# Delta rule on one core: diagonal blocks of 16 instead of 32 by substitution, the corner between them by products

## The chip, the cores and the metric

The program runs on one core of one Trainium2 chip. The time is device microseconds of one execution. Five engines matter: TensorE (PE; its weight loads are shown apart as PEld), VectorE (DVE), ScalarE (ACT), GpSimd (POOL) and SyncE (SP), which here issues DMAs. Each engine takes its instructions strictly in the order in which they stand in its queue; between engines, semaphores hold an instruction until what it reads is there.

## The reference

The program computes two blocks of a small model over 512 tokens. Only one part of the second block matters here, the gated delta rule, for eight heads of width 128. Its inner part, cut:

```python
decay = jnp.exp(jnp.where(causal, gc[..., :, None] - gc[..., None, :], -jnp.inf))
lmat = jnp.where(strict, jnp.einsum('bnhcd,bnhed->bnhce', k_beta, k) * decay, 0.0)
t_inv = lax.linalg.triangular_solve(eye + lmat, ..., left_side=True, lower=True, unit_diagonal=True)
u = jnp.einsum('bnhce,bnhed->bnhcd', t_inv, v_beta)
w = jnp.einsum('bnhce,bnhed->bnhcd', t_inv, k_beta * jnp.exp(gc)[..., None])
...
def step(state, xs):
    v_new = u_c - jnp.einsum('bhcd,bhde->bhce', w_c, state)
    o_c = jnp.einsum(..., q_c, state) + jnp.einsum(..., a_c, v_new)
    state = state * gl[..., None, None] + jnp.einsum('bhcd,bhce->bhde', k_c, v_new)
```

For each chunk of tokens a triangular matrix with ones on its diagonal has to be inverted (`t_inv`); then a state runs from chunk to chunk. The reference takes chunks of 64; the kernel takes chunks of 128, which gives the same result, so that a head has four chunks and each needs the inverse of a 128 x 128 triangle.

## The kernel before

The function that matters is `block2`. Its loop over eight heads, `for h in range(8)` (line 1444), emits for each head:

- Four projections by `K.gemm`, 24 products each (lines 313, 314 and 316, here called gemm products). Their weights come from `K.wtiles`: a DMA, a rounded copy `whi` on ScalarE (line 301), and the rest `wlo` by a subtraction on GpSimd (line 303). Three of the projections pass a convolution, `cv`, on VectorE (line 1290).
- The norm of q and k: transposes of `kq` into the PSUM buffers `ta`, sums of squares on ScalarE, some twenty small VectorE instructions (`rs_v` to `nbk`); `V` (line 1491); the decays `E`.
- Products of k with k and q (line 1502), of which VectorE makes `NU`, the strict triangle with its sign, and `Aq` (lines 1505 and 1507). All four chunks lie side by side in a tile.
- The inverse `D` of `I - NU`. Its four diagonal blocks of 32, of all four chunks at once, are gathered into `nd` [128, 4, 32] by four ScalarE copies and inverted by substitution in 31 steps of three VectorE instructions: a shuffle that gives every lane of 32 the row `i` (line 1519), a product (1521), a sum into `dc` (1522). A step i works on 4 x (31 - i) columns, from 124 down to 4.
- Then blocks are doubled, 32 to 64 to 128: ScalarE copies `dc` into `D`; VectorE transposes it into `Dt` (1527); products (1531), ScalarE copies `P1`, products (1538), ScalarE copies into `D`, transposes (1543), ScalarE copies `Dt6`, products (1548), ScalarE copies `P16`, products (1553), and VectorE copies the last corner into `D` (1554).
- The state over four chunks: products with `D` (1567), `vn` on ScalarE, products with `Aq`, `kd` and `kq`, and `Wc`, `O` and `S` on VectorE; at last the norm of `O`, its transposes, and `ya`.

The order on each engine is not this one. A scheduler with its own model of costs lays the instructions of neighbouring heads into each other: gemm products of later heads stand between the small products of this head, and while VectorE runs the substitution of one head, it also does the convolutions of a later head and the state of the head before. Two buffers stand for `D` (`Ds[h % 2]`), for `nd` and for most tiles of a head. Behind the heads come eight more projections, with no part in the delta rule, and an output stage that needs `ya` of all heads.

## Time and profile before

| | |
|---|---|
| runs shown | 2583.11, 2585.26, 2588.78 us; median 2585.26 us |
| profiled execution, first to last instruction | 2582.1 us |
| PE busy | 2421.6 us (94%) |
| VectorE busy | 1515.6 us (59%) |
| ScalarE busy | 986.7 us (38%) |
| GpSimd busy | 701.3 us (27%) |
| mean granted clock of TensorE | 0.972 |

The profile gives, for one execution, every instruction's engine, line, start and duration. A busy PE is not PE at its peak, since matmuls are pipelined and their ends are modelled. The granted clock is a share of 2.4 GHz; it takes two levels, 1.2 and 2.4 GHz, so that a mean between 0.5 and 1 says which part of a stretch ran at the lower one. The time of the profiled execution that is given is its span alone; the median of the runs lies 3.2 us above it. The shares are means over the whole program: the loop over heads fills the time from about 2110 to 2475 us. Many instructions in a product of two f32 operands are recorded twice, so a product there counts as two records.

### The profile page before, as it was taken

Reading aid. Unit: us, or ns where it says so; the run is one execution under the profiler, and the core shown is the slowest. Engines: PE = TensorE matmul, PEld = TensorE weight load, DVE = VectorE, ACT = ScalarE, POOL = GpSimd, SP = SyncE. Lnnn points to the kernel's source line nnn. Section 1 sums busy time; section 2 is a strip of 40 time slices with the busy share of each in tenths; the row PEclk is TensorE's granted clock in tenths of the full one; section 3 lists DMA queues with packets and bytes.
Section 4 is the critical chain, followed back from the end, with each engine's and each line's share of the span. In section 5 each row is a group of like instructions: output and inputs, shape, how many; then the busy total and the mean of one; then the engine's idle time right before and its main releaser. Section 6 shows DMA issues by size and latency. Waiting matters only on the chain.

```text
span 2582.1 us, 33519 instructions
## 1 busy us (share of the span) xinstructions
PE 2421.6 (94%) x12640; PEld 1977.7 (77%) x12640; DVE 1515.6 (59%) x3638; ACT 986.7 (38%) x1920; POOL 701.3 (27%) x313
## 2 busy tenths in 40 slices
PE   8899898999999999989989999999999998988897
PEld 4788777877888888867887788887777786666676
DVE  5857789788384452466875523335331248897854
ACT  4344433242132222344653423333444345554431
POOL 1221112222332223220013344443233342222242
PEclk9899999999999999999999999999999999998998
DMA  7311224325454331221002232223111231111131
GB/s 266 110 49 66 86 66 155 135 82 170 140 164 146 100 106 62 72 77 48 31 34 98 74 106 84 94 102 135 59 56 62 80 117 54 58 54 54 50 114 65
DMA packets 65889, 237.68 MB, mean 92 GB/s; under 512 B 7584, under 2 KB 10560, under 8 KB 50752
## 3 DMA queue, kind: packets, MB, share of 16 engines
q1 hardware_dynamic: 62848, 229.61, 26.2%
q10 hardware_dynamic: 2880, 5.94, 0.7%
q8 instruction: 100, 1.64, 0.3%
q14 instruction: 61, 0.50, 0.1%
HBM read 229.21 MB, written 6.31 MB: 91 GB/s over the span
## 4 chain that ended last, share of the span: by engine, by line
PE 70%; DVE 18%; ACT 3%; issue 2%; DMA 2%; DVEq 0%; ACTq 0%
PE mm L313 14%; PE mm L314 14%; PE mm L316 14%; PE mm L1134 4%; PE mm L1135 4%; PE mm L1136 4%; DVE ada_acc L365 2%; DVE dt L1521 2%; DVE dc L1522 2%; DMA adaraw<-in_ada_dram 2%; DVE row L1519 1%; PE lv L927 1%; DVE cv L1290 1%; PE mm L324 1%; PE mm L325 1%
## 5 line engine op out<-in xcount | busy, mean ns | idle before, releaser
L303 POOL TENSOR_TENSOR wlo<-wraw,whi 128x1024 fp32r<-128x1024 f32 (+2 forms) x301 | 686.8, 2283 | 1720.3 <-ACT whi L301 1486.1
L301 ACT ACTIVATE whi<-wraw 128x1024 fp32r<-128x1024 f32 (+2 forms) x301 | 299.8, 997 | 838.4 <-PE mm L314 361.4
L313 PE MATMUL mm<-fhi,whi 128*128 128x512 f32 (+1 forms) x1056 | 374.7, 358 | 1.9 <-ACT fhi L451 1.9
L314 PE MATMUL mm<-flo,whi 128*128 128x512 f32 (+1 forms) x1056 | 360.7, 357 | 0.0
L316 PE MATMUL mm<-fhi,wlo 128*128 128x512 f32 (+1 forms) x1056 | 321.6, 357 | 0.0
L313 PE MATMUL mm<-h2h,whi 128*128 128x512 f32 x584 | 243.8, 419 | 1.6 <-ACT h2h L451 1.6
L314 PE MATMUL mm<-h2l,whi 128*128 128x512 f32 x584 | 242.4, 416 | 0.0
L316 PE MATMUL mm<-h2h,wlo 128*128 128x512 f32 x584 | 241.3, 414 | 0.0
L313 PEld LDWEIGHTS mm<-fhi,whi 128*128 128x128 f32 x1056 | 198.5, 188 | 49.2 <-ACT fhi L451 2.7
L314 PEld LDWEIGHTS mm<-flo,whi 128*128 128x128 f32 x1056 | 198.7, 188 | 31.5 <-DVE flo L452 0.3
L365 DVE SCALAR_TENSOR_TENSOR ada_acc<-adaraw,silu_c,ada_acc 128x512 f32<-128x512 f32 x182 | 175.6, 965 | 33.1 <-DMA adaraw<-in_ada_dram 30.9
L316 PEld LDWEIGHTS mm<-fhi,wlo 128*128 128x128 f32 x1056 | 176.2, 190 | 17.7
L1134 PE MATMUL mm<-ffh,whi 128*128 128x512 f32 (+1 forms) x528 | 188.1, 358 | 1.1 <-ACT ffh L331 1.1
L1135 PE MATMUL mm<-ffl,whi 128*128 128x512 f32 (+1 forms) x528 | 188.7, 358 | 0.0
L1136 PE MATMUL mm<-ffh,wlo 128*128 128x512 f32 (+1 forms) x528 | 187.8, 357 | 0.0
L313 PE MATMUL mm<-hhi,whi 128*128 128x512 f32 (+1 forms) x488 | 173.9, 360 | 5.6 <-ACT F L884 3.7
L314 PE MATMUL mm<-hlo,whi 128*128 128x512 f32 x488 | 166.2, 359 | 0.7 <-DVE hlo L452 0.6
L1109 DVE SCALAR_TENSOR_TENSOR fft<-mm,sv,fft 128x511 f32<-128x511 f32 x66 | 43.5, 658 | 187.3 <-ACT fft L1108 187.3
L1138 DVE SCALAR_TENSOR_TENSOR x<-mm,mod_l,x 128x512 f32<-128x512 f32 x64 | 48.1, 751 | 165.3 <-PE mm L1136 165.3
L316 PE MATMUL mm<-hhi,wlo 128*128 128x512 f32 (+1 forms) x488 | 144.0, 362 | 0.0
L313 PEld LDWEIGHTS mm<-h2h,whi 128*128 128x128 f32 x584 | 113.9, 195 | 23.9 <-issue 1.8
L314 PEld LDWEIGHTS mm<-h2l,whi 128*128 128x128 f32 x584 | 114.4, 196 | 22.9 <-issue 1.6
(551 smaller groups left out, 4761.4 us busy)
## 6 DMA issues: line engine op xcount, KB each, us to landing
adaraw<-in_ada_dram SPq DMA_DIRECT2D x208, 256.0 KB, 3.0
wraw<-in_w_up_dram SPq DMA_DIRECT2D x44, 1024.0 KB, 4.7
wraw<-in_w_b_dram SPq DMA_DIRECT2D x40, 1024.0 KB, 4.9
wraw<-in_w_ev_dram SPq DMA_DIRECT2D x14, 1024.0 KB, 4.8
wraw<-in_w_dn_dram SPq DMA_DIRECT2D x16, 768.0 KB, 4.3
wraw<-in_w_dn_dram SPq DMA_DIRECT2D x16, 640.0 KB, 3.9
adaraw<-in_ada_dram SPq DMA_DIRECT2D x16, 512.0 KB, 10.0
wraw<-in_w_evo_dram SPq DMA_DIRECT2D x4, 1024.0 KB, 5.0
```

The costliest lines, as they stand in the source:

```text
L301: nc.scalar.activation(hi, raw[:, g], AF.Copy)
L303: nc.gpsimd.tensor_sub(lo, raw[:, g], hi.bitcast(F32))
L313: self.nc.tensor.matmul(p, whi[:, k, :], hhi[:, k, c0:c0 + n], start=k == 0, stop=False)
L314: self.nc.tensor.matmul(p, whi[:, k, :], hlo[:, k, c0:c0 + n], start=False, stop=False)
L316: self.nc.tensor.matmul(p, wlo[:, k, :], hhi[:, k, c0:c0 + n], start=False, stop=k == KT - 1)
L365: nc.vector.scalar_tensor_tensor(acc, raw, c[:, kk:kk + 1], acc, op0=OP.mult, op1=OP.add)
L1134: nc.tensor.matmul(p, whi[:, k, :], fhi[:, c:c + n], start=k == 0, stop=False)
L1135: nc.tensor.matmul(p, whi[:, k, :], flo[:, c:c + n], start=False, stop=False)
L1136: nc.tensor.matmul(p, wlo[:, k, :], fhi[:, c:c + n], start=False, stop=k == gn - 1)
L1138: nc.vector.scalar_tensor_tensor(xx[:, j], p, m[:, 40 + j:41 + j], xx[:, j], op0=OP.mult, op1=OP.add)
L1521: nc.vector.tensor_tensor(t, row, dc[:, :, i:i + 1].to_broadcast([128, 4, m]), op=OP.mult)
L1522: nc.vector.tensor_tensor(dc[:, :, i + 1:], dc[:, :, i + 1:], t, op=OP.add)
```

## The change

The four blocks of 32 on the diagonal are each cut into two blocks of 16 and a corner of 16 x 16. Both blocks of 16 go through one chain of 15 steps: the shuffle now gives the upper 16 lanes of each 32 their row `i` and the lower 16 their row `16 + i`. For this `nd` is first folded, by two masks, into `n16` [128, 4, 16]. The corner of every block of 32 is cut out by a mask (`nk`) and spread by four ScalarE copies into a block-diagonal tile `N` [128, 4, 128], of which there are two, zeroed once. After the chain `dh` is unfolded into `dc` by the two masks. Two groups of four products, `p1` and `p2`, multiply the inverses of the two blocks of 16 with the corner: `Dk` is the transpose of `dc`, `PX` spreads the result of `p1` block by block over 128 columns while reading it out of PSUM, and the result of `p2` is added to `dc`. From there on, from `D` and `Dt` to the end, the code is as before. The constants `d32` become one tile `dk`. The other edits take out comments, so that the lines of later code are shifted by some places.

```diff
-    A['d32'] = (i[:, None] % 32 == np.arange(32)).astype(f)
+    dk = np.zeros((128, 54), f)
+    dk[:, :16] = i[:, None] % 16 == np.arange(16)
+    dk[:, 16] = i % 32 < 16
+    dk[:, 17] = i % 32 >= 16
+    dk[:, 18:50] = (i[:, None] % 32 < 16) & (np.arange(32) >= 16)
+    dk[:, 50:] = i[:, None] // 32 == np.arange(4)
...
+        d16, m0, m1, corner, blk = dk[:, :16], dk[:, 16:17], dk[:, 17:18], dk[:, 18:50], dk[:, 50:54]
...
+        Ns = [dp.tile([128, 4, 128], F32, name=f"N{i}") for i in range(2)]
...
+            n16 = dp.tile([128, 4, 16], F32, name="n16", tag="n16", bufs=2)
+            nc.vector.tensor_scalar(n16, nd[:, :, 0:16], m0, None, op0=OP.mult)
+            nc.vector.scalar_tensor_tensor(n16, nd[:, :, 16:32], m1, n16, op0=OP.mult, op1=OP.add)
+            nk = dp.tile([128, 4, 32], F32, name="nk", tag="nk", bufs=2)
+            nc.vector.tensor_tensor(nk, nd, corner[:, None].to_broadcast([128, 4, 32]), op=OP.mult)
+            for b in range(4):
+                r = slice(32 * b, 32 * b + 32)
+                ND(N[r, :, r], nk[r])
+            dh = dp.tile([128, 4, 16], F32, name="dh", tag="dh", bufs=2)
+            nc.vector.tensor_copy(dh, d16[:, None].to_broadcast([128, 4, 16]))
+            for i in range(15):
+                m = 15 - i
+                row = dp.tile([128, 4, m], F32, name="row", tag="row", bufs=4)
+                nc.vector.stream_shuffle(row, n16[:, :, i + 1:], [i] * 16 + [16 + i] * 16)
+                t = dp.tile([128, 4, m], F32, name="dt", tag="dt", bufs=2)
+                nc.vector.tensor_tensor(t, row, dh[:, :, i:i + 1].to_broadcast([128, 4, m]), op=OP.mult)
+                nc.vector.tensor_tensor(dh[:, :, i + 1:], dh[:, :, i + 1:], t, op=OP.add)
             dc = dp.tile([128, 4, 32], F32, name="dc", tag="dc", bufs=2)
-            nc.vector.tensor_copy(dc, d32[:, None].to_broadcast([128, 4, 32]))
-            for i in range(31):
-                m = 31 - i
-                row = dp.tile([128, 4, m], F32, name="row", tag="row", bufs=4)
-                nc.vector.stream_shuffle(row, nd[:, :, i + 1:], [i] * 32)
-                t = dp.tile([128, 4, m], F32, name="dt", tag="dt", bufs=2)
-                nc.vector.tensor_tensor(t, row, dc[:, :, i:i + 1].to_broadcast([128, 4, m]), op=OP.mult)
-                nc.vector.tensor_tensor(dc[:, :, i + 1:], dc[:, :, i + 1:], t, op=OP.add)
+            for k, m in enumerate((m0, m1)):
+                nc.vector.tensor_scalar(dc[:, :, 16 * k:16 * k + 16], dh, m, None, op0=OP.mult)
+            Dk = dp.tile([128, 4, 32], F32, name="Dk", tag="Dk", bufs=2)
+            nc.vector.transpose(Dk.rearrange("p a b -> p (a b)"), dc.rearrange("p a b -> p (a b)"))
+            p1 = K.pt("tb")
+            for c in range(4):
+                nc.tensor.matmul(p1[:, c * 32:c * 32 + 32], N[:, c], Dk[:, c], start=True, stop=True)
+            PX = dp.tile([128, 4, 4, 32], F32, name="PX", tag="PX", bufs=1)
+            nc.vector.tensor_tensor(PX, p1[:, None, :128].rearrange("p o (c j) -> p c o j", c=4).to_broadcast([128, 4, 4, 32]),
+                                    blk[:, None, :, None].to_broadcast([128, 4, 4, 32]), op=OP.mult)
+            p2 = K.pt("tb")
+            for c in range(4):
+                nc.tensor.matmul(p2[:, c * 32:c * 32 + 32], PX[:, c].rearrange("p b j -> p (b j)"), dc[:, c], start=True, stop=True)
+            nc.vector.tensor_tensor(dc, dc, p2[:, :128].rearrange("p (a b) -> p a b", a=4), op=OP.add)
```

Up to the first head's substitution each engine's order is that of before; from there the scheduler lays the heads into each other in another way. VectorE's queue of before, at the end of the fifth head's substitution (an entry is line, operation, result and sources, result's size; `tb` and `ta` are PSUM buffers):

```order
L1527 STREAM_TRANSPOSE Dt<-dc 128x128
L1491 TENSOR_TENSOR V<-ta,ik 128x512
L1507 TENSOR_TENSOR Aq<-ta,E 128x256
L1290 SCALAR_TENSOR_TENSOR cv<-mm,sv,cv 128x511
L1515 COPY dc<-d_14818 128x128
L1290 SCALAR_TENSOR_TENSOR cv<-mm,sv,cv 128x510
L1505 SCALAR_TENSOR_TENSOR NU<-ta,nbk,E 128x128 x2
L1507 TENSOR_TENSOR Aq<-ta,E 128x256
L1290 SCALAR_TENSOR_TENSOR cv<-mm,sv,cv 128x509
L1554 COPY D_16811<-tb 64x4x64
L1519 STREAM_SHUFFLE row<-nd 128x124
```

The same place in the changed kernel, where the lines 1544, 1559 and 1586 are the transposes `Dk` and `Dt` and the last copy into `D`, and line 1554 is now the sum of `p2` into `dc`:

```order
L1544 STREAM_TRANSPOSE Dk<-dc 128x128
L1532 COPY dh<-dk 128x64
L1549 TENSOR_TENSOR PX<-tb,dk 128x512
L1554 TENSOR_TENSOR dc<-dc,tb 128x128
L1559 STREAM_TRANSPOSE Dt<-dc 128x128
L1586 COPY D_16811<-tb 64x4x64
L285 TENSOR_SCALAR rs_v<-dss 128x8
L287 TENSOR_SCALAR rs_i<-rs_v 128x8
L289 TENSOR_SCALAR rs_j<-rs_i 128x8
L293 TENSOR_TENSOR rs_t<-rs_j 128x8
```

The next head's `V`, `NU` and `Aq` and the convolutions stood between `Dt` and the copy into `D`; now nothing stands there, and the small instructions of the next head's norm begin behind the copy.

PE's queue of before, at the end of the third head's substitution (the first of the products of line 1531 is the last row; line 1296 is a transpose):

```order
L1296 MATMUL ta<-cst,vc 128x128 x4
L313 MATMUL mm<-h2h,whi 128x512
L314 MATMUL mm<-h2l,whi 128x512
L316 MATMUL mm<-h2h,wlo 128x512
L313 MATMUL mm<-h2h,whi 128x512
L314 MATMUL mm<-h2l,whi 128x512
L1502 MATMUL ta<-kq 128x256 x2
L1296 MATMUL sm<-cst,O 128x128 x4
L1531 MATMUL tb<-Dt,NU 32x32
```

The same place in the changed kernel (lines 1547 and 1553 are `p1` and `p2`, 1304 a transpose, 320, 321 and 323 the gemm, 1563 the products that were at 1531):

```order
L323 MATMUL mm<-h2h,wlo 128x512
L1547 MATMUL tb<-Dk,N_16813 128x32 x4
L1304 MATMUL ta<-cst,kq 128x128 x8
L1553 MATMUL tb<-dc,PX 128x32 x4
L320 MATMUL mm<-h2h,whi 128x512
L321 MATMUL mm<-h2l,whi 128x512
L323 MATMUL mm<-h2h,wlo 128x512
L320 MATMUL mm<-h2h,whi 128x512
L1563 MATMUL tb<-Dt,NU 32x32
```

Two groups of products came in ahead of the old ladder, and the transposes of the next head's k and q, which stood some twenty gemm products earlier, now stand between these groups; in the other heads up to seven gemm products stand there.

## Rows read from the trace of the kernel before

**Rows 1.** Windows, three stretches: us; PE, PEld, DVE, ACT, POOL busy (count); PEclk; DMA

```profile
2122.10:2162.20 40.10, 34.15 (x169) 26.29 (x168) 33.62 (x166) 19.47 (x48) 10.12 (x5) 0.87 0.23 72
2162.20:2425.30 263.10, 231.38 (x1253) 173.68 (x1252) 226.24 (x1176) 136.34 (x376) 57.84 (x24) 0.94 0.17 56
2425.30:2453.80 28.50, 25.24 (x155) 18.13 (x154) 25.32 (x131) 11.65 (x31) 7.18 (x3) 1.00 0.11 39
```

**Rows 2.** The chain of waits from 2122 to 2446 us, shares by line

```profile
by line: DVE dt L1521 14.0%; DVE dc L1522 12.5%; DVE row L1519 10.9%; DVE cv L1290 8.1%; PE mm L314 7.3%; PE mm L313 7.1%; PE mm L316 7.0%; PE ta L1502 5.1%; PE tb L1531 3.9%; DVE E L1496 2.4%; DVE Wc L1565 1.5%; PE sm L1577 1.4%; PE tb L15
```

**Rows 3.** Windows: two with a substitution, then four from its end on

```profile
2162.80:2194.20 31.40, 26.44 (x135) 20.70 (x134) 30.68 (x167) 16.44 (x45) 7.33 (x3) 0.99 0.15 51
...
2420.60:2445.20 24.60, 21.41 (x116) 15.52 (x116) 22.22 (x135) 8.77 (x22) 4.83 (x2) 1.00 0.19 69
...
2150.40:2162.80 12.40, 12.02 (x73) 8.45 (x74) 6.54 (x29) 6.29 (x17) 2.36 (x1) 0.72 0.22 65
2194.20:2208.20 14.00, 14.00 (x78) 9.29 (x77) 6.53 (x31) 6.63 (x19) 2.35 (x1) 0.66 0.14 37
2238.40:2248.20 9.80, 9.80 (x77) 6.93 (x77) 6.56 (x30) 5.70 (x17) 2.39 (x1) 1.00 0.37 123
...
2445.20:2453.80 8.60, 8.53 (x71) 5.80 (x70) 6.33 (x18) 4.18 (x14) 2.35 (x1) 1.00 0.01 2
```

**Rows 4.** Timeline, third head's doubling: start, us, engine, line, operation, tiles, count [idle before]

```profile
2238.45 0.31 DVE L1527 STREAM_TRANSPOSE Dt<-dc 128x128 f32<-128x128 f32 x1
...
2238.98 1.67 PE L1531 MATMUL tb<-Dt,NU 32*32 32x32 f32 x16
...
2243.90 1.13 PE L1502 MATMUL ta<-kq 128*128 128x256 f32 x4
...
2244.96 0.67 PE L1548 MATMUL tb<-Dt,NU 64*64 64x64 f32 x8
...
2247.17 0.42 DVE L1554 COPY D<-tb 64x256 f32<-64x256 f32 x1 [1.16 <-PE tb L1553]
```

**Rows 5.** Timeline of DVE, wide steps of a substitution, then steps of half the width

```profile
2248.57 0.27 DVE L1521 TENSOR_TENSOR dt<-row,dc 128x124 f32<-128x124 f32 x1
...
2248.77 0.28 DVE L1519 STREAM_SHUFFLE row<-nd 128x116 f32<-128x116 f32 x1
2248.96 0.27 DVE L1522 TENSOR_TENSOR dc<-dc,dt 128x124 f32<-128x124 f32 x1
...
2224.99 0.23 DVE L1519 STREAM_SHUFFLE row<-nd 128x64 f32<-128x64 f32 x1
2225.12 0.23 DVE L1522 TENSOR_TENSOR dc<-dc,dt 128x76 f32<-128x76 f32 x1
```

**Rows 6.** Groups by line, 2060 to 2460 us: busy us, mean ns, idle before, releasers

```profile
L1441 ACT ACTIVATE nd<-NU 32x128 f32<-32x128 f32 x32 | 9.8, 306 | 0.5
...
L1574 DVE TENSOR_TENSOR O<-O,sm 128x128 f32<-128x128 f32 x22 | 6.1, 279 | 2.3 <-PE sm L1570 2.2
...
L1491 DVE TENSOR_TENSOR V<-ta,ik 128x512 f32<-128x512 f32 x8 | 5.5, 682 | 0.0
```

**Rows 7.** Timeline of POOL and DVE around one of GpSimd's subtractions

```profile
2252.26 2.38 POOL L303 TENSOR_TENSOR wlo<-wraw,whi 128x1024 fp32r<-128x1024 f32 x1 [8.65 <-ACT whi L301]
2252.38 2.39 DVE L1521 TENSOR_TENSOR dt<-row,dc 128x108 f32<-128x108 f32 x1
```

**Rows 8.** Product and sum: groups by line (mean ns), then by tile (ns least/median/most)

```profile
L1521 DVE TENSOR_TENSOR dt<-row,dc 128x124 f32<-128x124 f32 (+30 forms) x248 | 77.0, 310 | 0.2
L1522 DVE TENSOR_TENSOR dc<-dc,dt 128x124 f32<-128x124 f32 (+30 forms) x248 | 73.4, 296 | 2.4
...
L1521 DVE TENSOR_TENSOR dt<-row,dc x248: 155/217/2419, 2122.4 to 2444.7; 128x124 f32<-128x124 f32 x4, 128x116 f32<-128x116 f32 x4, 128x108 f32<-128x108 f32 x4, 128x100 f32<-128x100 f32 x4
L1522 DVE TENSOR_TENSOR dc<-dc,dt x248: 153/221/2401, 2123.0 to 2445.0; 128x124 f32<-128x124 f32 x4, 128x116 f32<-128x116 f32 x4, 128x108 f32<-128x108 f32 x4, 128x100 f32<-128x100 f32 x4
```

**Rows 9.** A window behind the heads, where PE has gemm products alone

```profile
2475.00:2485.00 10.00, 10.00 (x45) 8.10 (x44) 6.29 (x10) 6.45 (x12) 3.19 (x3) 1.00 0.80 315
```

More of the change, by code (lines that the diff above doesn't have):

```diff
@@ L1436, in block2 @@
         Ds = [dp.tile([128, 4, 128], F32, name=f"D{i}") for i in range(2)]
-        for D in Ds:
+        Ns = [dp.tile([128, 4, 128], F32, name=f"N{i}") for i in range(2)]
+        for D in Ds + Ns:
             nc.vector.memset(D, 0.0)
@@ L1507, in block2 @@
                 nc.vector.tensor_tensor(Aq[:, c0:c0 + 2], pgv[:, :, 1], E[:, c0:c0 + 2], op=OP.mult)
[L1509 removed]
+            D, N = Ds[h % 2], Ns[h % 2]
             nd = dp.tile([128, 4, 32], F32, name="nd", tag="nd", bufs=2)
```

6 lines of the change are left out of this document (3 added, 3 removed).

## Prediction

> **What bounds the kernel now.** The change touches eight heads of the second block, some 330 us of a span of 2582.1 us, so I read that stretch alone. First the stretches of time [rows 1]. From the end of the first head's copy into `D` (line 1554, 2162.2) to the end of the seventh's (2425.3) lie six like cycles of 263.1 us, 43.9 us each. In them PE is busy 88% and VectorE 86% (226.24 us, 37.7 us a cycle, so 6.1 us idle): two engines near full, neither quite. The chain of waits decides between them [rows 2]: the three lines of the substitution (1519, 1521, 1522) make 37.4% of it, some 121 us of 324 or 15 us a head, each of the three gemm lines only about 7%. VectorE bounds this stretch, and mostly by the work that the change shortens.
>
> Then where VectorE rests. While a substitution runs it is full (30.68 us of 31.40 in the second head). Behind it lies what I call the tail, 9.8 to 14.0 us in the first six heads, of which it works about 6.5 [rows 3]. The tail is a ladder between PE and ScalarE: transposed blocks `Dt`, products (1531), `P1`, products (1538), copies, transposes (1543), `Dt6`, products (1548), `P16`, products (1553), the copy into `D`. In the third head it runs from 2238.45 to 2247.59, 9.1 us, at full clock [rows 4]. The order of before fills it: behind `Dt`, VectorE does `V`, `NU`, `Aq` and convolutions of the next head, and the copy into `D` stands at the end of that. So the next substitution starts 0.6 us after the copy.
>
> **What is removed.** The 31 steps become 15, and these have the widths of the old steps 17 to 31. So the sixteen widest steps go: 48 instructions, 124 to 64 columns. Their durations are 0.28 to 0.23 us, but a start follows the last start sooner: 0.20 us behind a product of 124 columns, 0.19 behind a shuffle of 116, 0.13 behind a shuffle of 64 [rows 5]. A mean of 0.172 us gives 48 x 0.172 = 8.3 us a head.
>
> The Trainium skill, VectorE: DVE Perf Modes, "The DRAIN you can't avoid", says that the next op does not start until the pipe of the last is empty, so that each op costs about its duration. By that the 48 would give 12.1 us instead of 8.3, and the added ops 2.9 instead of 1.8. The rows show starts 0.2 us apart under durations of 0.28, so I sum by starts and keep the rule as a rival.
>
> **What is added on VectorE**, a head, by start spacing: `n16`, two ops of 64 columns, 0.3; `nk`, 128 columns, 0.2; `dh` for the old start copy, nothing net; two half copies into `dc`, 0.3; the transpose `Dk`, 0.23 (0.31 long, as `Dt` [rows 4]); `PX`, 512 columns out of PSUM, 0.6 (as `V`, 0.682 long [rows 6]); the sum into `dc` out of PSUM, 0.2 (as `O`, 0.279 long [rows 6]). Together 1.8 us. The bounds for the seven, which the trace lacks, are 1.2 (all at the 0.13 spacing but `PX`) and 2.9 us (full durations).
>
> **GpSimd's part.** GpSimd runs 24 `wlo` subtractions in the six cycles [rows 1], four a head of 2.4 us, and a VectorE op that meets one lasts as long: 2252.26 to 2254.64 there, 2252.38 to 2254.77 here [rows 7]. The product and the sum have means of 310 and 296 ns over medians of 217 and 221; over 248 each that is 41.7 us, 5.2 a head [rows 8]. Removing ops does not remove these, since each subtraction finds some op in the shorter chain too. Only because VectorE will rest more (below) do I take a fifth off, 1.0 us; bounds 0 and 2.
>
> VectorE's own time per cycle is then 37.7 - 8.3 + 1.8 - 1.0 = 30.2 us, with 28 and 32 as ends.
>
> **What is lengthened, and what lies under the tail.** The order is the other half of the sum. In the changed kernel the copy into `D` follows `Dt` at once in most heads, and the norm, `V` and `NU` of the next head, which lay under the tail, stand behind it; the transposes of the next head's k and q have moved on PE to `p1` and `p2`. VectorE, in order, waits at that copy with nothing to do, and the whole queue for the next substitution waits with it.
>
> The longer tail: `Dk` 0.31; `p1`, eight records on PE, between 0.67 (eight of 64 x 64) and 1.13 (four of 128 x 256) [rows 4], taken 0.75 for the small column count; `PX` 0.68; `p2` 0.75 (the transposes in front of it pass while `PX` runs); the sum 0.28; semaphores some 0.05 at each of five places: 3.0 us to `Dt`. Then the old ladder: 8.6 us, as its last instance had (2445.2 to 2453.8 [rows 3], against 9.1 in the third head). That is 11.6 us, of which VectorE works 1.6 us, and 4.2 in two of six heads where convolutions stand there: 9.1 idle in the mean.
>
> Preparation: from the copy into `D` to the first `n16` I count `vn`, two products, the state copy, the next products, `V` before the second pair of `ta` products, `NU`, `Aq`, four copies `nd` (0.31 each [rows 6]) and 6.2 us of VectorE work: 7.6 us, 1.4 idle. While the chain runs: 0.7 idle as before. ScalarE's four copies into `N`, 1.2 us, run beside the chain; ScalarE is busy 52% [rows 1].
>
> Clock: three of the first six tails ran at a granted mean of 0.66 to 0.72, hence partly at 1.2 GHz, and took 12.4 to 14.0 us, against 9.8 at 1.00 [rows 3]; PE had waited in the chain windows before (busy 26.44 us of 31.40). I expect as many: 3 us in three of eight heads, 1.2.
>
> Idle: 9.1 + 1.4 + 0.7 + 1.2 = 12.4 us instead of 6.1. **A cycle is 30.2 + 12.4 = 42.6 us instead of 43.9**: the substitution gives 6.5 us net and 1.0 us from GpSimd, and the uncovered tail takes 6.3 back.
>
> **The ends of the stretch.** First head, from the first shuffle to its copy into `D`: 40.1 us [rows 1]. Its chain window of 28.3 (2122.1 to 2150.4) becomes 28.3 - 8.3 + 0.5, less one subtraction of 2.0 that now falls behind it, 18.5; the tail 11.6 + 0.5: 30.6, a gain of 9.5. The 68 gemm products that now stand ahead of `p1` need 68 x 0.22 = 15.1 us (45 in 10 us [rows 9]) and fit. Last head: 28.5 us [rows 1]; it had its `NU` ready under the tail of the seventh and no longer has: 7.8 + (22.2 of work [rows 3] - 8.3 + 0.5 - 0.9 + 1.5 waiting) 15.0 + 11.9 = 34.7, a loss of 6.2. After its last transposes, four more products stand ahead than before: 0.9 us. From there PE is full, so the shift reaches the end.
>
> Sum: -6 x 1.25 - 9.5 + 6.2 + 0.9 = -9.9 us. The profiled span becomes 2572.2 us; the median of the runs lies 3.2 us over the profiled span, so 2575 us.
>
> **Rivals.** *The uncovered tail costs more than the chain gives* (slower). Place: VectorE's queue at the copy into `D`, with norm, `NU` and the substitution behind it. For it: 6.3 us of idle are put against 7.5 us of work, and each 1 us more of idle per head costs 8 us; from 1.25 us on there is no gain. If the tail takes 14 us, the longest row, and no subtraction is escaped: 31.2 + 15.4 = 46.6 us a cycle, +16.5, first head -6.5, last +8.2, +0.9: 2604 us. Against it: at full clock the ladder took 8.6 to 9.1. The longer tail has two more places at which PE waits, and the three slow tails show that waits there go with the lower clock. The Trainium skill, TensorE: Matmul & The Clock Gate, "HAM oscillation", says the same: bursts of products between waits start throttled each time.
>
> *PE becomes the bound* (faster). PE's busy time is 231.38 / 6 = 38.6 us a cycle [rows 1], with `p1` and `p2` 40.1. If waits overlap so well that VectorE no longer counts, six cycles gain 3.75 each: -22.5 - 9.5 + 0.9 = -31, 2554 us. The order speaks against it: work has left the tail.
>
> *Ops cost their durations* (faster): 2.7 us more per head, 22 us: 2553 us. The rule is the one of the Trainium skill above; the spacing in the rows denies it.
>
> *The loss equals the gain* (no change): idle 1.25 us higher than I sum, 2585 us. That the change is not made can be left out: the order shows 15 steps and two new groups of products in all eight heads.
>
> **How the numbers follow.** Forecast 0.48 (0.08 of it above 2580), slower rival 0.27 (0.05 of it within 5 us), PE as the bound 0.12, durations 0.05, no change 0.08. A difference of 0.2%, 5.2 us, is about what a measurement of this kernel can tell from none. Faster: 0.40 + 0.12 + 0.05 = 0.57; same: 0.08 + 0.05 + 0.08 = 0.21; slower 0.22. The range runs from the two fast rivals, a little below, to the slow one: 2550 to 2602.
>
> **What the changed profile would show.** Right: 15 steps in a chain window of some 22 us with little idle; VectorE idle for 8 to 10 us ahead of each copy into `D`; cycles of 41 to 44 us; four `wlo` a head, two or three of them met. Wrong: chain windows with much idle (then PE or ScalarE paces them), tails of over 13 us or a granted clock under 0.8 in most of them (slower), or `NU` ready by the time of the copy (faster).

## The result and the profile after

The changed kernel takes **2616.3 us** (median of 6 runs, 2608.9 to 2621.2) against 2590.6 us (6 runs, 2583.1 to 2602.9) of the kernel before beside it: the ratio is 1.0091, with a 95% interval of 1.0063 to 1.0119. The change costs 0.9%, where I had forecast a gain of 0.4%; the time lies 14 us above my range. The profiled execution spans 2613.8 us, 31.7 more than that of before.

The three stretches of [rows 1], now from the first shuffle (2125.1) over the seven copies into `D` to the eighth (windows, same columns):

```profile
2125.10:2161.60 36.50, 31.60 (x148) 24.32 (x147) 18.15 (x80) 16.93 (x43) 7.09 (x3) 0.69 0.16 56
2161.60:2434.10 272.50, 250.13 (x1321) 193.34 (x1321) 171.08 (x818) 141.79 (x388) 57.19 (x24) 0.87 0.15 52
2434.10:2476.90 42.80, 38.48 (x199) 28.66 (x198) 23.44 (x124) 17.54 (x52) 7.10 (x3) 0.84 0.10 28
```

VectorE's busy time in the six cycles fell from 226 to 171 us, just as intended. The cycles became longer, 45.4 us for 43.9, and the granted clock fell from 0.94 to 0.87, in the first head from 0.87 to 0.69. The chain of waits over these heads tells the same (the counterpart of [rows 2]): the three substitution lines, 1536, 1538 and 1539, have 13.0% of it where they had 37.4, and the gemm lines lead.

```profile
by line: PE mm L321 10.7%; PE mm L320 10.6%; PE mm L323 10.0%; DVE dt L1538 5.1%; DVE dh L1539 5.0%; DVE cv L1298 4.9%; PE tb L1563 4.5%; PE ta L1304 4.4%; DMA E<-grd 4.3%; PE ta L1511 3.6%; PE tb L1553 3.0%; DVE row L1536 2.9%; PE tb L1547
```

Two heads show what happens. Windows of the fifth: chain up to `Dk`, `Dk` to `Dt`, ladder up to the copy, preparation up to the next first shuffle.

```profile
2306.40:2325.30 18.90, 16.99 (x79) 13.19 (x79) 18.25 (x96) 9.49 (x21) 4.80 (x2) 1.00 0.22 64
2325.30:2328.90 3.60, 3.26 (x26) 3.10 (x27) 1.33 (x4) 2.47 (x5) 0.00 (x0) 1.00 0.61 255
2328.90:2337.50 8.60, 8.60 (x73) 5.97 (x72) 0.74 (x4) 6.65 (x27) 2.37 (x1) 1.00 0.00 1
2337.50:2347.10 9.60, 9.60 (x53) 7.79 (x52) 8.79 (x42) 6.33 (x20) 2.38 (x1) 1.00 0.19 55
```

Its parts make 40.7 us, all at the full clock. The first head, same parts without the preparation:

```profile
2125.10:2141.60 16.50, 12.00 (x52) 9.33 (x50) 16.12 (x74) 7.98 (x11) 4.75 (x2) 0.93 0.22 69
2141.60:2147.70 6.10, 5.69 (x22) 5.16 (x23) 1.35 (x6) 1.72 (x3) 0.00 (x0) 0.50 0.36 150
2147.70:2161.60 13.90, 13.90 (x76) 9.83 (x75) 0.68 (x3) 7.23 (x30) 2.34 (x1) 0.50 0.00 0
```

Here the ladder takes 13.9 us for 8.6, with PE busy for all of it, at 0.50, that is at 1.2 GHz. The sixteen products on line 1563, first in the first head, then in the fifth (timeline of PE; compare [rows 4]):

```profile
2148.89 2.42 PE L1563 MATMUL tb<-Dt,NU 32*32 32x32 f32 x16
...
2329.47 1.67 PE L1563 MATMUL tb<-Dt,NU 32*32 32x32 f32 x16
```

What stood ahead of the slow stretch, in the timeline of the first head:

```profile
2136.71 0.39 PE L320 MATMUL mm<-h2h,whi 128*128 128x512 f32 x1
...
2137.64 2.34 POOL L310 TENSOR_TENSOR wlo<-wraw,whi 128x1024 fp32r<-128x1024 f32 x1 [6.29 <-ACT whi L308]
2137.68 2.32 DVE L1539 TENSOR_TENSOR dh<-dh,dt 128x4 f32<-128x4 f32 x1
...
2141.56 0.30 DVE L1544 STREAM_TRANSPOSE Dk<-dc 128x128 f32<-128x128 f32 x1
...
2142.01 0.82 PE L1547 MATMUL tb<-Dk,N 128*128 128x32 f32 x3 [4.90 <-DVE dh L1532]
```

PE has done its last gemm product at 2137.1. Next in its queue stands `p1`, which needs `Dk`; a GpSimd subtraction holds the last step of the chain for 2.3 us, as in [rows 7], and convolutions stand ahead of `Dk`. PE waits 4.9 us, and all the products that could fill the time stand behind `p1`. It waits so in heads 7 (3.9) and 8 (4.0) too.

The three other slow ladders have no such wait ahead of them. In heads 2 and 5 PE waits nearly alike at `p1`, 1.2 and 0.9 us, and one ladder runs at 0.69, the other at 1.00. In heads 3 and 6 it doesn't wait at `p1` at all. It waited 2.8 and 2.0 us within the chain, for steps of VectorE that GpSimd's subtractions held up, and the ladders ran at 0.68 and 0.50. Head 6, its two waits, then `Dk` to `Dt` and the ladder:

```profile
2352.95 0.49 PE L1609 MATMUL sm<-vn,kd 128*128 128x128 f32 x2 [2.79 <-DVE O L1606]
...
2366.57 0.44 PE L1304 MATMUL sm<-cst,O 128*128 128x128 f32 x2 [2.03 <-DVE O L1623]
```

```profile
2368.60:2375.20 6.60, 6.60 (x30) 6.21 (x29) 1.38 (x5) 2.59 (x7) 2.35 (x1) 0.50 0.11 43
2375.20:2388.50 13.30, 13.30 (x70) 8.86 (x69) 0.89 (x4) 6.63 (x28) 0.00 (x0) 0.50 0.00 0
```

### Where the 31.7 us come from

In the eight heads let T be the stretch, PE's rest T less its busy time, and the clock's loss T times (1 - clock), which counts half of the time at the lower clock as lost. What is left is PE's work at the full clock. The whole stretch, before and after:

```profile
2122.10:2453.80 331.70, 290.78 (x1574) 218.10 (x1573) 285.18 (x1470) 167.47 (x455) 75.14 (x32) 0.93 0.17 56
```

```profile
2125.10:2476.90 351.80, 320.21 (x1665) 246.32 (x1664) 212.68 (x1019) 176.25 (x483) 71.38 (x30) 0.85 0.15 50
```

| us | T | PE's rest | clock's loss | PE's work |
|---|---|---|---|---|
| before | 331.7 | 40.9 | 23.2 | 267.6 |
| after | 351.8 | 31.6 | 52.8 | 267.4 |

So the heads lose 20.1 us: PE rests 9.3 us less, and the clock takes 29.6 us more (the clock has two digits, so each loss is good to 1.8 us). The split is good to several us, not better: the sixteen products above take 2.42 us at the lower clock for 1.67, less than twice as long, so where much runs at it the loss comes out too high and the work too low. The work is equal only because gemm products have left the heads, 713 for 750, while `p1` and `p2` came in.

The rest of the 31.7: 3.0 us ahead of the first shuffle (`V` stands 1.3 us later already; behind it `n16`, `nk` and a convolution are new), and 8.6 us behind the last copy into `D`, where 30 gemm products more stand than before, 6.6 us at 0.22 each [rows 9]. The other 7 of the 37 are done ahead of the first shuffle.

### The profile page after: what moved, and what is told of

Its sections match the earlier page's. It is cut to its first block, busy times and chain, and to the rows that moved or that the text cites. A ratio compares the mean times of both kernels' runs of the same rounds, so it can differ in the third digit from the quotient of the medians.

```text
span 2613.8 us, 33376 instructions
## 1 busy us (share of the span) xinstructions
PE 2461.1 (94%) x12768; PEld 2008.3 (77%) x12768; DVE 1444.2 (55%) x3192; ACT 998.3 (38%) x1952; POOL 699.2 (27%) x313
## 4 chain that ended last, share of the span: by engine, by line
PE 72%; DVE 14%; ACT 3%; DMA 3%; issue 2%; DVEq 0%; ACTq 0%
PE mm L321 14%; PE mm L320 14%; PE mm L323 14%; PE mm L1141 4%; PE mm L1143 4%; PE mm L1142 4%; DVE ada_acc L372 2%; DMA adaraw<-in_ada_dram 2%; PE lv L934 1%; PE mm L331 1%; PE mm L332 1%; PE mm L334 1%; PE ta L1304 1%; DVE dt L1538 1%; DVE dh L1539 1%
## 5 line engine op out<-in xcount | busy, mean ns | idle before, releaser
L320 PE MATMUL mm<-h2h,whi 128*128 128x512 f32 x584 | 249.4, 429 | 1.6 <-ACT h2h L458 1.6
L323 PE MATMUL mm<-h2h,wlo 128*128 128x512 f32 x584 | 248.4, 426 | 0.0
L372 DVE SCALAR_TENSOR_TENSOR ada_acc<-adaraw,silu_c,ada_acc 128x512 f32<-128x512 f32 x182 | 184.0, 1011 | 34.4 <-DMA adaraw<-in_ada_dram 32.2
L1116 DVE SCALAR_TENSOR_TENSOR fft<-mm,sv,fft 128x511 f32<-128x511 f32 x66 | 43.4, 658 | 189.4 <-ACT fft L1115 189.4
```

Source lines behind the costliest of these rows:

```text
L320: self.nc.tensor.matmul(p, whi[:, k, :], hhi[:, k, c0:c0 + n], start=k == 0, stop=False)
L323: self.nc.tensor.matmul(p, wlo[:, k, :], hhi[:, k, c0:c0 + n], start=False, stop=k == KT - 1)
L372: nc.vector.scalar_tensor_tensor(acc, raw, c[:, kk:kk + 1], acc, op0=OP.mult, op1=OP.add)
L1116: nc.vector.scalar_tensor_tensor(tv[:, 1:], p[:, :n - 1], cw[:, j:j + 1], tv[:, 1:], op0=OP.mult, op1=OP.add)
```

## The experiments

A ratio is that to the kernel before, run beside on the same chip, with its 95% interval. Differences in us are between medians; the kernels ran on several chips, on which the kernel before had medians from 2585.8 to 2595.1 us, so where the ratios give another difference it is named. Kernels named a_ start from the kernel after, b_ from before. The scheduler lays the order of each kernel anew, unless the text says that it is unchanged.

### The corner, the short chain and the copy

*a_nocorner* takes the corner out of the change (its lines from `nk` to the copies into `N`, and from `Dk` to the sum into `dc`); *b_corner* puts it behind the whole chain of before:

```diff
+        N = dp.tile([128, 4, 128], F32, name="N")
+        blk = dp.tile([128, 4], F32, name="blk")
-        for D in Ds:
+        for D in Ds + [N, blk]:
             nc.vector.memset(D, 0.0)
...
+            Dk = dp.tile([128, 4, 32], F32, name="Dk", tag="Dk", bufs=2)
...
+            nc.vector.tensor_tensor(dc, dc, p2[:, :128].rearrange("p (a b) -> p a b", a=4), op=OP.add)
```

> The kernel after without the corner: no nk, no copies into N, no Dk, p1, PX, p2 and sum, so the blocks of 32 lack their corner and the output is another. What is left of the change is the 15-step chain alone. If the round trip of the corner is what costs (5.4 us from Dk to Dt in the mean, and 2.7 us of PE a head), this is some 43 us faster than after: 2570 us or less. If the wait of PE behind a short chain is what costs, the wait only moves from p1 to the first products of the doubling, the ladder still runs at half clock in four or more heads, and no more than 20 to 30 us come back: 2586 to 2596.

> The kernel before, its 31-step chain whole, with the corner's round trip added behind it on blocks that are zero (Dk, p1, PX, p2 and the sum into dc; N and blk hold zeros, so the sum adds nothing). It prices the corner alone under a chain that is as long as before. If the round trip costs by itself wherever it stands: 5 us a head, 2625 to 2635 us. If PE has gemm products to do under the longer chain and the clock stays, it costs what I had summed, 3.0 us a head with the ladder uncovered as in after, or less: 2600 to 2615.

Measured: a_nocorner 2593.1 us, 1.0013 (0.9998 to 1.0027); b_corner 2626.5 us, 1.013 (1.010 to 1.016). The corner costs 23 us behind the short chain and 36 behind the long one, against the 24 (8 x 3.0) that I had summed (20 and 34 by the ratios). The other half is the surprise: the 15-step chain alone, with 48 instructions of the substitution fewer and no corner, is worth nothing. PE waits elsewhere: at `Dt` or at the last transposes of `O`, for 3.7 to 4.6 us in five heads.

*a_dact* and *a_lo_dve_dact* move the last copy into `D` off VectorE:

```diff
-            nc.vector.tensor_copy(D[:64, :, 64:], p2[:64, :256].rearrange("p (a b) -> p a b", a=4))
+            nc.scalar.activation(D[:64, :, 64:], p2[:64, :256].rearrange("p (a b) -> p a b", a=4), AF.Copy)
```

> The kernel after, with the last copy into D on ScalarE instead of VectorE, so that VectorE no longer stands at it with its queue behind it. My forecast had laid the uncovered ladder to that wait. If it is so, the norm, V and NU of the next head slide under the ladder and a cycle of 45.4 us loses 3 us or more: 2616 less 20 to 30, 2586 to 2596 us. If what follows in VectorE's queue needs the copy's result anyway, or PE and its clock set the time, it stays within 8 us of 2616.

Measured: 2627.6 us, 1.0132 (1.0105 to 1.0158), 11 us slower than after. VectorE's longest waits in the heads, first of after, then of a_dact (engine, line, what it waited for: us, times, longest):

```profile
DVE D L1586 <- PE tb L1585: 66.1, 8, 13.2
DVE rs_v L285 <- ACT junk L1479: 19.8, 3, 11.1
```

```profile
DVE rs_v L285 <- ACT junk L1479: 58.1, 6, 13.9
DVE O L1604 <- PE sm L1602: 34.4, 5, 17.5
```

The wait has moved to the norm of the next head, whose squares on ScalarE come from the transposes of k and q. In after, PE has these behind `p1`. My forecast put the rest under the ladder down to VectorE's wait at the copy; the copy was only the first instruction to stand there. (PE's order in the heads is another here, so the 11 us are not the price of the copy alone.)

### GpSimd's subtractions

In the first head PE's wait came with a held step, one that lasts as long as the GpSimd subtraction beside it. *a_lo_dve* and *b_lo_dve* put the subtractions of the eight heads on VectorE:

```diff
+    lo_eng = 'gpsimd'
...
-                nc.gpsimd.tensor_sub(lo, raw[:, g], hi.bitcast(F32))
+                getattr(nc, self.lo_eng).tensor_sub(lo, raw[:, g], hi.bitcast(F32))
...
+        K.lo_eng = 'vector'
         for h in range(8):
...
+        K.lo_eng = 'gpsimd'
         for j in range(8):
```

> The kernel after, with the wlo subtractions of the eight heads on VectorE instead of GpSimd; nothing else is edited (the planner may order anew). Theory held: in the kernel after, a GpSimd subtraction holds a step of the chain for 2 us, twice in heads 1, 3, 6, 7 and 8; PE meanwhile stands at p1 with nothing else in its queue (4.9, 3.9 and 4.0 us in heads 1, 7 and 8), and the granted clock goes to half for the ladder behind it (105.8 us at half between 2118 and 2500 us, 44.4 in the kernel before). With no subtraction on GpSimd the gaps ahead of p1 should be under 1.5 us in all heads, the time at half clock under 50 us, and the kernel 20 to 30 us faster than after: 2586 to 2596 us, although VectorE gets 32 subtractions (estimate 1.3 us each, from twice the 0.69 us of one with 512 columns) for some 40 us of held steps. Rival: the clock falls because the ladder's own products are thin and wait for each other, whoever subtracts: half clock stays at 90 to 120 us, and the time within 6 us of after's 2616.

> The kernel before, with the same subtractions on VectorE: the partner of the run above, so that the change can be read with and without GpSimd's subtractions. Held steps are three a head there, 6.3 us; the four subtractions cost VectorE some 5.2 us a head by estimate. Theory held: a gain of about 1 us a head, 2575 to 2590 us; and the change (blocks of 16) is then worth 0 to 10 us against this kernel instead of costing 26. Rival (the change costs because of its longer tail alone, whatever GpSimd does): the change costs 20 to 30 us between these two kernels also.

Measured: **a_lo_dve 2557.5 us, 0.9882 (0.9863 to 0.9902)**, faster than both kernels; b_lo_dve 2591.4 us, 1.0007 (0.9990 to 1.0024). a_lo_dve came out some 30 us under my expectation, and the change is worth 34 us here. The stretch of the heads in a_lo_dve:

```profile
2126.60:2414.60 288.00, 280.77 (x1668) 217.66 (x1666) 222.38 (x1045) 176.11 (x483) 14.61 (x6) 0.98 0.18 61
```

PE's work is 275.0 us, its rest 7.2 and the clock's loss 5.8 (31.6 and 52.8 in after). Its only wait at `p1` (line 1550 there) of any size is 2.1 us:

```profile
PE sm L1612 <- DVE O L1609: 3.3, 2, 1.9
PE tb L1550 <- DVE Dk L1547: 2.1, 1, 2.1
```

The edit also made the scheduler lay the order anew. *a_lo_both* tells the two apart: the order on PE, VectorE and ScalarE is that of a_lo_dve word for word, and GpSimd does each subtraction once more for nobody. *b_lo_both* is the same on b_lo_dve, and *a_both_8ths* does the unread subtraction in eight parts.

```diff
+                if self.lo_eng == 'vector':
+                    nc.gpsimd.tensor_sub(self.unread, raw[:, g], hi.bitcast(F32))
```

> The kernel a_lo_dve (2557 us) with each subtraction done once more on GpSimd, into a tile that nobody reads. The order of the instructions on PE, VectorE and ScalarE is that of a_lo_dve, word for word; only GpSimd has 32 subtractions in the heads again, one beside each. Held theory (GpSimd's subtractions hold steps of the short chain, PE waits at p1, the clock falls): held steps come back, one or two a chain, gaps of over 1.9 us ahead of p1 in three or more heads (there was one of 2.1), 60 us or more at half clock between 2110 and 2500 us (there were 13.7), and the time rises by 25 to 50 us to 2582 to 2607. Rival (a_lo_dve won because the planner laid the same work in another order): the time stays within 8 us of 2557.

> The kernel b_lo_dve (2591 us; the 31-step chain, the subtractions of the heads on VectorE) with each subtraction done once more on GpSimd for nobody. The order on PE is the same word for word, on VectorE and ScalarE but for a few lines ahead of the first head. It is the mirror of a_lo_both, which lost 79 us to the same 32 subtractions. If these cost as much wherever they meet a chain of VectorE: 2650 us or more. If they cost what VectorE is held (some 3 steps of 2.1 us a head, 45 to 55 us) and PE has gemm products beside the long chain, so that the clock stays near b_lo_dve's 55 us at half: 2620 to 2645. If VectorE's rests take them up, under 2610.

> The kernel a_lo_both (2636 us), order unchanged, with the unread subtractions on GpSimd in eight parts of 128 columns. It tells the length of one hold from GpSimd's traffic. If the length of a hold counts (VectorE gets through between the parts, as a_eighths had it, 23 us under after): no held steps, 2560 to 2590 us. If GpSimd's traffic costs VectorE the same in sum: 2620 us or more.

Measured: a_lo_both 2636.3 us, 1.0164 (1.0144 to 1.0184), **79 us slower at an unchanged order**; b_lo_both 2649.2 us, 1.0241 (1.0216 to 1.0265), 58 us slower; a_both_8ths 2604.8 us, 1.0069 (1.0043 to 1.0094), 47 us slower (73, 61 and 48 us by the ratios). The first lost more than I had expected, the last came out between its two cases. Heads of a_lo_both, then of a_both_8ths:

```profile
2143.30:2503.30 360.00, 323.57 (x1665) 247.16 (x1664) 258.62 (x1045) 176.97 (x483) 78.56 (x30) 0.85 0.15 51
```

```profile
2132.10:2465.90 333.80, 313.42 (x1664) 239.18 (x1663) 241.87 (x1044) 176.99 (x482) 114.09 (x198) 0.87 0.16 54
```

PE's work is again 270 us in both. In a_lo_both the rest is 36.4 and the clock's loss 54.0; in a_both_8ths 20.4 and 43.4. A held step in a_lo_both (VectorE's timeline, 0.17 us unheld):

```profile
2156.02 2.00 DVE L1544 TENSOR_TENSOR dt<-row,dh 128x28 f32<-128x28 f32 x1
...
2159.08 0.17 DVE L1545 TENSOR_TENSOR dh<-dh,dt 128x28 f32<-128x28 f32 x1
```

So what an order in which PE nearly never waits had gained is lost again through delays of VectorE of a few us a head (in a_lo_both its busy time rises from 222.4 to 258.6 us, 4.5 a head). But the mirror runs took away the explanation that I held by then, that GpSimd makes the change a loss: the kernel before pays 58 us for the same subtractions. What settles it are kernels in which GpSimd keeps them and holds nobody for long, in eight parts of 128 columns. In these the order on PE, VectorE and ScalarE is that of after, or of before, word for word. *a_eighths* does so for the heads; *a_eighths_sga* and *b_eighths_sga* also for the eight weight tiles behind them, whose subtractions are made ahead and still fall into heads 7 and 8.

```diff
-                nc.gpsimd.tensor_sub(lo, raw[:, g], hi.bitcast(F32))
+                for k in range(0, KT, KT // self.parts):
+                    nc.gpsimd.tensor_sub(lo[:, k:k + KT // self.parts], raw[:, g, k:k + KT // self.parts], hi[:, k:k + KT // self.parts].bitcast(F32))
...
+        K.parts = 8
         for h in range(8):
```

> The kernel after, each subtraction of the eight heads on GpSimd done in eight parts of 128 columns. GpSimd's busy time is the same or somewhat more; each part takes 0.3 us or a little over. If a held step waits for the one GpSimd instruction that it meets, holds of 2 us become holds of 0.3 us, but there are eight times as many and the sum stays: 2605 to 2625 us. If VectorE gets through between the parts, the chain windows with two holds (16.5, 21.5, 21.5, 15.6 and 12.7 us) lose 2 to 4 us, the gaps ahead of p1 and half the time at half clock go: 2570 to 2595 us.

> The kernel a_eighths (2593 us), with the subtractions of the eight weight tiles behind the heads in eight parts too. Its waits of 4.0 us ahead of p1 stood in heads 7 and 8 alone, where whole subtractions still ran on GpSimd. If they make those waits: waits under 2 us there, ladders of 8 to 10 us instead of 12.3 and 15.5, 2575 to 2585 us. If the planner's place of p1 makes them whatever GpSimd does, 2589 to 2597.

> The kernel before, with GpSimd's subtractions of the heads and of the eight weight tiles behind them in eight parts of 128 columns: the partner of a_eighths_sga (2583 us). The kernel before has 26 held VectorE instructions in its heads, some 47 us over what they need, and VectorE bounds it; it keeps its gemm products beside the 31-step chain. If short subtractions hold nobody and the holds were on VectorE's path: 2545 to 2560 us, faster than the changed kernel in the same form, and the change is then a loss of 25 us or more there. If PE's waits take the place of the holds (b_lo_dve, without holds, had 2591 with 39 us of subtractions put on VectorE): 2575 to 2590 us, level with a_eighths_sga.

Measured: a_eighths 2593.2 us, 1.0015 (0.9997 to 1.0033); a_eighths_sga 2583.4 us, 0.9967 (0.9948 to 0.9986); **b_eighths_sga 2557.7 us, 0.9879 (0.9858 to 0.9900)**. So GpSimd's holds cost each kernel some 32 us, at an unchanged order. The two last have no VectorE instruction over 1.5 us in their heads, and the change still costs 26 us between them, as it does with whole subtractions. Heads of a_eighths_sga, then of b_eighths_sga:

```profile
2127.80:2451.50 323.70, 306.09 (x1663) 233.29 (x1662) 197.79 (x1020) 176.10 (x483) 104.22 (x240) 0.89 0.16 55
```

```profile
2126.10:2441.30 315.20, 294.44 (x1575) 219.63 (x1574) 264.06 (x1471) 168.39 (x455) 109.60 (x252) 0.92 0.17 59
```

PE's rest is 17.6 against 20.8 us, the clock's loss 35.6 against 25.2. In the heads it is the pattern of before and after, smaller: with the change PE rests less, and the clock costs more. But that makes only 8.5 of the 21.2 us between the two profiled spans (each the longest execution of its kernel); 1.7 lie ahead of the heads and 11.0 behind them, where 32 gemm products more stand (7.0 us). Head 8 of a_eighths_sga waits 3.3 us ahead of `p1` with no held step, and its ladder takes 15.5 us; so the place of `p1` makes such a wait without a hold too.

### Three more

*a_lo_dve_sga* and *b_lo_dve_sga* set `K.lo_eng` back only behind the eight tiles that follow the heads.

> The kernel a_lo_dve, with the subtractions of the eight weight tiles behind the heads on VectorE too. These are made three tiles ahead, so some of them still fell into heads 7 and 8 on GpSimd: there a_lo_dve had its 3 held steps, its one gap of 2.1 us ahead of p1 and 13.7 us at half clock, with ladders of 12.4 and 8.4 us. If they are the cause there too, the held steps go to 0, the half clock to under 5 us, head 7's ladder to 8.5 to 9.5, and the time to 2545 to 2553 us. If the clock in head 7 falls for another reason, it stays at 2554 to 2560 with a ladder of 12 us.

> The kernel before with the subtractions of the heads and of the eight tiles behind them on VectorE: the partner of a_lo_dve_sga, for the size of the change when GpSimd leaves the heads alone. VectorE's 31-step chain bounds it: 2585 to 2595 us, and the change is then worth 35 to 45 us.

Measured: 2558.4 us, 0.9867 (0.9842 to 0.9892), and 2584.5 us, 0.9974 (0.9958 to 0.9989). The held steps are gone, but there is no gain over a_lo_dve; the change is worth 26 us in this pair. In a_lo_dve_sga PE rests 1.0 us in all eight heads, and yet two ladders are slow, the fourth and the seventh with 12.1 and 11.5 us. These, after the whole stretch:

```profile
2136.30:2422.20 285.90, 284.86 (x1680) 220.18 (x1679) 221.10 (x1051) 176.07 (x483) 0.00 (x0) 0.97 0.19 64
...
2269.10:2281.20 12.10, 12.10 (x72) 7.83 (x71) 5.80 (x24) 6.25 (x17) 0.00 (x0) 0.72 0.04 10
2376.40:2387.90 11.50, 11.50 (x71) 7.70 (x70) 5.15 (x21) 6.93 (x29) 0.00 (x0) 0.69 0.01 2
```

In the seventh the clock is at 0.99 for the first 4.4 us of the ladder and at 0.50 for the other 7.1, with PE busy throughout. So the rival in the expectation of a_lo_dve, that the clock falls in the ladder itself, whoever subtracts, is not out: these two bear it out.

*a_lo_dve_dact* (both edits), *a_nocorner_lo_dve* and *b_corner_lo_dve* (with the subtractions on VectorE):

> Both edits: the kernel a_lo_dve with the last copy into D on ScalarE. PE is busy 98% of the six cycles of a_lo_dve, so if PE bounds it there is no more to gain than its idle 4 us and the first and last head: 2550 to 2560 us. If VectorE's wait at the copy still counts (preparation took 9 to 13.5 us in four of seven heads), 2540 us or less.

> The kernel a_lo_dve without the corner (no nk, copies into N, Dk, p1, PX, p2, sum; the blocks of 32 lack their corner and the output is another). With a_nocorner (2593 us) it prices the corner and the short chain without GpSimd's subtractions. If PE bounds these kernels, the corner is worth its products, 128 records of some 0.17 us: 22 us, 2535 us; and the short chain alone, which was worth nothing (a_nocorner 2593 against 2590 before), is worth 50 us or more here. If instead the round trip from Dk to Dt sets it, 8 x 4.1: 2525 us or less. If neither, it stays near 2557.

> The kernel before with the corner's round trip on zero blocks behind the whole chain (b_corner, 2626 us) and the subtractions of the heads on VectorE. It asks whether the corner is cheap by itself (5 us between a_lo_dve and a_nocorner_lo_dve) or only behind a short chain, where PE bounds the kernel. If it is cheap wherever GpSimd doesn't subtract: 2591 to 2600 us, beside the 2591 of b_lo_dve. If behind a long chain VectorE's wait for the round trip is on the path: 2615 to 2630.

Measured: 2558.5 us, 0.9856 (0.9835 to 0.9877), so the copy does nothing here either; 2552.8 us, 0.9839 (0.982 to 0.9858), so the corner costs 5 us where PE is fed (11 by the ratios); 2617.7 us, 1.0116 (1.0079 to 1.0153), 26 us for the corner behind the long chain.

*a_lead* and *a_lead_lo_dve* write the gemms and convolutions of the next head ahead of `Dk`, as a function `lead`, so that `p1` stands behind them on PE:

```diff
+            nxt = lead(h + 1) if h < 7 else None
             Dk = dp.tile([128, 4, 32], F32, name="Dk", tag="Dk", bufs=2)
```

> The kernel after, GpSimd's subtractions as they are; the four gemms and convolutions of the next head are written ahead of Dk in the code, so that p1 stands behind all 96 gemm products of the next head on PE: 20 products later in head 7, 14 in head 4, 5 in head 1, 2 in head 8, 0 to 9 in the others. It fills PE's wait ahead of p1 without touching GpSimd. If the wait ahead of p1 brings the clock down, head 7 (a gap of 3.9 us, 20 products are 4.4 us) runs its ladder in 8.6 to 10 us instead of 12.5, head 1 (4.9 us, 1.1 filled) and head 8 stay slow, and the kernel comes to 2600 to 2612 us. If the clock falls without that wait, head 7's ladder stays over 12 us and the time is 2616 or more, since p1 comes later.

> Both: the next head's gemms ahead of Dk, and the subtractions of the heads on VectorE. PE was busy 98% of the six cycles of a_lo_dve and ran 13.7 us at half clock, so by the held theory there is little left: 2550 to 2560 us. If the place of p1 counts beside GpSimd's subtractions, 2545 or less.

Measured: 2613.7 us, 1.0101 (1.0070 to 1.0131), and 2557.1 us, 0.9885 (0.9858 to 0.9911): no difference in the whole. Head 7, on which the question rested, did what was expected. Chain, `Dk` to `Dt`, ladder, in after and then in a_lead:

```profile
2398.70:2414.30 15.60, 12.08 (x60) 9.28 (x59) 15.30 (x84) 7.27 (x17) 4.83 (x2) 1.00 0.22 71
2414.30:2421.70 7.40, 7.02 (x29) 6.15 (x30) 3.64 (x11) 1.23 (x4) 0.00 (x0) 0.60 0.37 135
2421.70:2434.10 12.40, 12.40 (x76) 8.70 (x75) 2.02 (x5) 5.59 (x17) 2.35 (x1) 0.69 0.00 1
```

```profile
2412.90:2429.80 16.90, 14.87 (x72) 11.33 (x71) 16.49 (x87) 8.00 (x20) 4.69 (x2) 1.00 0.18 63
2429.80:2437.90 8.10, 6.21 (x41) 5.54 (x42) 4.84 (x11) 2.83 (x7) 2.09 (x2) 1.00 0.39 130
2437.90:2446.00 8.10, 8.10 (x72) 5.47 (x70) 1.38 (x8) 6.06 (x26) 0.37 (x1) 1.00 0.01 2
```

The wait at `p1` is gone and the ladder runs at the full clock. But heads 4 and 6, which had `Dk` to `Dt` in 5.0 and 6.6 us, now take 6.9 and 12.4, and the clock falls in other ladders instead: the fourth and fifth, at 1.00 in after, run at 0.50 and 0.67.

### What the runs show together

| us | before, 31 steps | after, 15 steps and corner | the change | of it the clock's loss |
|---|---|---|---|---|
| subtractions whole on GpSimd | 2590.6 | 2616.3 | +26 | +23 |
| in eight parts on GpSimd | 2557.7 | 2583.4 | +26 | +7 |
| on VectorE | 2591.4 | 2557.5 | -34 | -28 |
| on both | 2649.2 | 2636.3 | -13 | -3 |

By the ratios the change is +24, +23, -32 and -20 us. For the last column each execution has its span and its mean granted clock; span times (1 - clock) is its loss over the whole program, and the column has the differences of the medians (for the kernel before, of its 96 executions beside the other runs). Upper two rows: one order on PE, VectorE and ScalarE down each column; lower two: another (in b_lo_both but for six places on VectorE and a few on ScalarE ahead of the heads). At neither order do GpSimd's holds turn the sign. It turns with the order and with the work on VectorE. In the first and third rows the clock holds most of the difference, in the second and fourth little of it.

The change takes some 70 us off VectorE (285.2 to 212.7 us busy in the heads) and puts round trips with PE in their place. My reading, which no run shows by itself: where VectorE has extra work to do, 39 us of subtractions (32 of 1.22 us, 25 of them within the heads), the freed time takes it up and the change gains; where it has none, the freed time turns into rests, and the work of `p1` and `p2` and what the clock takes are left as the price. PE has the same 266 to 276 us of work in all these kernels but those without a corner (252 and 255) or with the corner added to the long chain (287 and 273) and b_lo_both (263).

Shown: the sums of rest and clock; the price of a disturbed order and, at an unchanged one, of GpSimd's holds; that these aren't what turns the sign. No run changes the clock alone, but the executions of one kernel differ in it at the same program: over 96 of the kernel before the span goes from 2574.6 us at 0.975 to 2602.6 at 0.964, and with each us of the clock's loss go 0.8 us of span (correlation 0.92). Not shown: what brings the clock down in a given ladder, since it fell behind long waits at `p1` (heads 1, 7 and 8 of after), behind shorter ones elsewhere (heads 3 and 6) and with none (a_lo_dve_sga); why the order that the scheduler makes with the subtractions on VectorE keeps PE fed (in it `p1` stands up to 34 gemm products later than in after, in three of seven heads the next head's preparation lies under the ladder). A run at that order without the subtractions on VectorE, which would tell order and extra work apart, was not made.

## Why the prediction was wrong

**Right, or better than forecast.** VectorE's own time: 28.5 us a cycle, where I had 30.2 (28 to 32). The chain window: 18.7 us in the mean of the six heads, where I had some 22, with little rest (18.25 of 18.90 us busy in the fifth). Steps follow each other by start, not by duration; the rival on durations is out (in the first head `dt` with 60 columns starts at 2125.32 and the next at 2125.83, 0.51 us for three instructions of 0.21). GpSimd's escape, which I took at 1.0 us a head, was more: held instructions in the heads fell from 26 to 12, of some 2.1 us over their own time, 3.7 us a head.

**The serial part.** `Dk` to `Dt`: 3.0 forecast; 3.6 us in the fifth head, 5.4 in the mean of the six. Of that, `p1` and `p2` took 2.7 us of PE a head (19.1 us over seven), not 1.5. Preparation, copy to `n16`: 7.6 forecast, 8.1 to 10.9 measured; in the sixth VectorE works 8.79 of 9.60 us, since convolutions stand there that I had counted elsewhere. These two put nearly 4 us a cycle on the path (2.4 and, at a mean of 9.0, 1.4), about what the better chain gave.

**The step that failed is the clock term.** I took 3 us in three of eight heads, 1.2 us in the mean. Six of eight ladders ran slow: 13.9, 11.7, 10.5, 13.3, 12.4 and 13.6 us, against 9.0 and 8.6 in the fourth and fifth, at 1.00. That is 22.6 us more than at 8.8 each, 2.8 a head. In the whole stretch the clock's loss grew by 29.6 us, more than the 20.1 that the heads lost, where I had put it at as much as before. Where nearly all of it ran at the full clock the cycle was as forecast or better: 40.4 and 41.9 us up to the fourth and fifth copies, for 42.6. The reason for "as many" slow tails was wrong. I looked for PE's waits under the chain in sum, which did fall (40.9 to 31.6 us), and the slow ladders became more. I didn't ask where each wait would stand: in heads 1, 7 and 8 no more spread through a chain of 30 us with gemm products between, but in one piece ahead of `p1`, at the door of the ladder, which is now on the path. That is half of the six; why the clock fell in heads 2, 3 and 6 stays open.

The Trainium skill, TensorE: Matmul & The Clock Gate, "HAM oscillation", which I cited for the slow rival, describes products in bursts that each start throttled after a wait, there for a DMA. The first head agrees: a wait of 4.9 us, then 0.50 for the 20 us up to the copy. The two slow ladders of a_lo_dve_sga, with no wait over 0.4 us in the heads, it doesn't tell of.

**The ends.** First head: 36.5 us, a gain of 3.6 for 9.5, by the same slow ladder and a `Dk` to `Dt` of 6.1 us. The gemm products ahead of `p1` fitted under the chain, as I had said; they ran out 4.9 us ahead of it. Last: 42.8, a loss of 14.3 for 6.2 (preparation 11.6, `Dk` to `Dt` 4.9, ladder 13.6). Behind the heads 8.6 for 0.9: I had counted the four products ahead of one place, not the 30 that no longer fitted in ahead of them. The 3.0 us ahead of the first shuffle I had not counted.

**The rivals.** The slow one happened, with its mechanism (a ladder of 11.6 us in the mean, up to 13.9, and nothing over it; from `Dk` to the copy some 16 us a cycle, where it had 14) and its sign, at 2604 for 2616; its place, VectorE's queue at the copy, was wrong as far as a_dact, with its other order, can tell. PE as the bound is what a_lo_dve became: the gemm lines lead its chain of waits (49.9%), and the time, 2557, is near the 2554 of that rival. That the numbers meet is luck: VectorE does 39 us more there, at another order.

## What to carry to other kernels

Before counting what a shorter chain saves on the engine that bounds, look at what the other engine has queued ahead of the product that waits for the chain's end: here it had nothing left for 3.9 to 4.9 us in three heads. Count the work that the change adds to that engine as well; here it pushed 30 gemm products out behind the heads. Where PE is near full, split a stretch into its work, its rest and T times (1 - clock): in the change under study the last term held most of the result, in the pair with eight parts it didn't. Long two-input operations of GpSimd beside a VectorE chain are worth cutting up first: that alone, at an unchanged order, gave 32 us to the kernel before, more than the change under study in any form but one. Moving them to VectorE gave it nothing (2591.4).
